# A two-layer decoder trunk: attention steps of a head pair placed inside later projections, and an MLP product with a 512-column operand

## The chip, the cores and the metric

The kernel runs on one core of a Trainium2 chip. The metric is the device time of one execution in microseconds (us); shorter is better. The core's engines work in parallel: TensorE (PE, with its weight loads counted apart as PEld), VectorE (DVE), ScalarE (ACT), GpSimd (POOL) and SyncE (SP), which starts most of the transfers from memory (DMA). Each engine takes its instructions in a fixed order and waits on semaphores for the others.

## The reference

256 tokens (SEQ) of width 1024 (D) pass through two layers. Everything is float32.

```python
def reference(x, ...):
    h = x
    for layer in range(2):
        hn = rms_norm(h, norm_gain[layer, 0])
        if layer == 0:
            h = h + stick_breaking_attention(hn, sb_w_qkv[0], sb_w_o[0])     # 16 heads of 64
        else:
            h = h + nsa_attention(hn, nsa_w_q[0], nsa_gate_b[0], nsa_w_o[0], shared)
        h = h + sqrelu_mlp(rms_norm(h, norm_gain[layer, 1]), mlp_w1[layer], mlp_w2[layer])
        if layer == 0:
            shared = nsa_shared_kv(h, kv_norm, nsa_w_kv, cmp_pos, cmp_w1, cmp_w2)
    return rms_norm(h, final_norm)

def sqrelu_mlp(x, w1, w2):              # w1: 1024 x 4096, w2: 4096 x 1024
    h = relu(x @ w1)
    return (h * h) @ w2

# stick-breaking attention, per head and block of 128 queries
z = q @ k.T * scale
log_1m = where(causal, log_sigmoid(-z), 0)
excl = cumsum(log_1m, reverse=True) - log_1m
a = where(causal, exp(log_sigmoid(z) + excl), 0)
o = a @ v
```

The attention of layer 1 (`nsa_attention`) is a sparse one with three branches: compressed blocks, selected blocks and a window. The change touches it only in how its tiles are allotted.

## The kernel before

**Exact products.** A float32 number is written as a high part, rounded to the type that PE multiplies in one pass, and a low part, the rest. A product of two such numbers is three matmuls, `mm3` (lines 127 to 130): high by high, high by low, low by high. Lines 128, 129 and 130 of the profile are these three. The first operand is the one loaded into PE (a block of 128 x 128), the second streams through it by columns. For projections and the MLP's first product the loaded operand is a weight block and the columns are the 256 tokens, kept transposed in tiles `xh` and `xl` (`xt_tiles` line 196, written by `xt_evac` lines 186 to 194: ACT writes the high part, DVE the low part, for each of eight blocks `k` of 128 rows of D).

**Weights.** All weights are read once, in order, as blocks of up to 1 MB. `fetch` (72) starts a transfer from SP into one of three `raw` buffers. `split` (82) makes half a block ready: an ACT cast (line 92) writes `wh`, a DVE subtraction (line 93) writes `wl`; there are three buffers of each, and after the second half the next block is fetched. `W(i)` waits until block i is split, and calls of `step()` scattered through the code place the splitting of later blocks, up to two blocks ahead. Where a `step()` stands sets where these two instructions (about 1 us each) stand in the order of ACT and DVE.

**Layer 0's attention** (`layer0`, 291 to 427). After the projection of all values `v`, a loop runs over eight head pairs. `proj` (350) makes queries and keys of a pair: 8 blocks k x 2 x `mm3` of 256 columns into one PSUM bank, and a DVE pass that writes `qkT` (line 359). `scores` (362) makes the scores `z` on PE, and then a long chain: two DVE passes clip and mask them into `e` (378, shown as sbe), ACT takes exp (382) and log (383) into `s` (sbs), DVE does a running sum (`tensor_tensor_scan`, 384) and a subtraction (385), and ACT takes the last exp. `turn` (389) transposes the result on PE by 128 x 128 blocks, and ACT (400) and DVE (398) copy one head each into `at` (sbt). `values` (403) multiplies with `v` into `po`, and `o_evac` (199 to 201) writes the high and low part of the output `oT`. The loop's order is written out by hand:

```python
proj(0); scores(0); proj(1); scores(1)
for p in range(NP - 2):
    proj(p + 2); turn(p); scores(p + 2); values(p)
```

`out_proj` (210) follows, the output projection with four weight blocks; its `hooks`, called at a step (i, n, kk), place the last two pairs' turn and values and the first half of the next transposed activations (`xt_tr` 176, `xt_evac`) between its products.

**The MLP** (`mlp`, 229 to 289; used in both layers) goes through 16 chunks of 256 hidden columns. `first(c)` (252) multiplies: 8 blocks k x 2 halves f x `mm3`, 48 matmuls of 256 columns, into one PSUM bank `pu` with the two halves side by side. Then ACT writes relu of it (`mr`, 264), DVE the product of `pu` and `mr` (`ms`, 266), ACT and DVE the high and low part `hh`, `hl` (270, 271). `second` (236) multiplies a chunk by w2: 24 matmuls of 512 columns, into four banks `acc` that stay for the whole MLP. The second product of a chunk follows the first product of the next chunk, so a chunk's result is needed one first product later; the last two chunks' second products come together at the end. In chunk 0 the second half of the transposed activations (blocks k 4 to 7) is only made inside the loop, at k = 2.

**Memory.** Large tiles share six equal buffers of 8 KB per partition (`big`, line 53); PSUM has eight banks in two groups of four (`bank` and `bank2`, lines 56 to 60). The order on each engine is fixed when the program is built: the framework takes the instructions in program order, by dependencies and buffers, and may pull some of them ahead.

Of the kernel before, what the change touches and what calls it, by code (L numbers as in the profile page):

```python
# [7 lines left out]
F32 = mybir.dt.float32  # L8
# [6 lines left out]
P = 128  # L15
# [24 lines left out]
def hybrid_kernel(ctx, tc, x, eye, gcols, gfin, wqk, wv, wo0, wkv, wqa, wqb, wqc, wo1, w1, w2, cw1, cw2, cpos, gate_b, consts, out):  # L40
# [10 lines left out]
        return a.bitcast(F32)  # L51

    def big(shape, dt, name):
        return cp.tile(shape, dt, tag="e", name=name, bufs=6)

    def bank(name, dt=F32):
        return ps.tile([P, 512], dt, tag="a", name=name, bufs=4)
# [1 line left out]
    def bank2(name):  # L59
        return ps.tile([P, 512], F32, tag="z", name=name, bufs=4)  # L60
# [66 lines left out]
    def mm3(o, a, b, first, last):  # L127
        nc.tensor.matmul(o, a[0], b[0], start=first, stop=False, skip_group_check=True)  # L128
        nc.tensor.matmul(o, a[0], b[1], start=False, stop=False, skip_group_check=True)  # L129
        nc.tensor.matmul(o, a[1], b[0], start=False, stop=last, skip_group_check=True)  # L130

    def mm(o, a, b, first, last):
        nc.tensor.matmul(o, a, b, start=first, stop=last, skip_group_check=True)  # L133

    def tok(xt, k, t):
        return xt[0][:, k, t * P:(t + 1) * P], xt[1][:, k, t * P:(t + 1) * P]

    def both(xt, k):
        return xt[0][:, k, :], xt[1][:, k, :]

    def cut(hl, a, b):
        return hl[0][:, a:b], hl[1][:, a:b]
# [51 lines left out]
                                               op0=OP.mult, op1=OP.subtract)  # L194

    def xt_tiles(tag):
        return big([P, NK, T * P], F32R, f"xh{tag}"), big([P, NK, T * P], F32R, f"xl{tag}")

    def o_evac(oT, po, p):
        nc.scalar.copy(oT[0][:, p, :], po[:, 0:T * P])  # L200
# [28 lines left out]
    def mlp(layer, gi, xt, mid, ap):  # L229
# [21 lines left out]

        def first(c):
            w = W(wa[c])
            pu = bank2("pu")
            for k in range(NK):
                if c == 0 and k == 2:
                    xt_evac(xt_tr(1), 1, gi, xt)
                if k % 4 == 0 and (c or k):
                    step()
                for f in range(2):  # L260
                    mm3(pu[:, f * 256:(f + 1) * 256], cut(w, k * 256 + f * P, k * 256 + (f + 1) * P),
                        both(xt, k), f == 0 and k == 0, k == NK - 1)
            r = ap.tile([P, 512], F32, name="mr")
            nc.scalar.activation(r, pu, AF.Relu)
            s = ap.tile([P, 512], F32, name="ms")
            nc.vector.tensor_mul(s, pu, r)  # L266
# [24 lines left out]
    def layer0(ap):  # L291
# [54 lines left out]
        oT = big([P, NP, T * P], F32R, "oT_h"), big([P, NP, T * P], F32R, "oT_l")  # L346

        live = {}

        def proj(p):  # L350
            qk = bank("qk")
            w = W(i_qk[p])
            for k in range(NK):
                if k % 4 == 0:
                    step()
                mm3(qk[:, 0:256], cut(w, k * 256, k * 256 + P), both(xt, k), k == 0, k == NK - 1)
                mm3(qk[:, 256:512], cut(w, k * 256 + P, k * 256 + 2 * P), both(xt, k), False, k == NK - 1)
            qkT = ap.tile([P, 2, T * P], F32, name="qkT", bufs=3)
            nc.vector.tensor_mul(qkT, qk.rearrange("p (a q) -> p a q", a=2), rbq)
            live[p] = qkT  # L360
# [41 lines left out]

        def values(p):
            a = live.pop(p)
            po = bank2("po") if p >= NP - 2 else bank("po")
            for b in range(2):
                for hd in range(2):
                    r = slice(hd * DH, (hd + 1) * DH)
                    cs = slice(p * P + hd * DH, p * P + (hd + 1) * DH)
                    q = (slice(0, 256), slice(256, 384))[b]  # L410
                    mm(po[r, b * P:2 * P], v[:, b, cs], a[:, hd, q], b == 0, b == 1)
            o_evac(oT, po, p)

        proj(0)
        scores(0)
        proj(1)
        scores(1)
        for p in range(NP - 2):
            proj(p + 2)
            turn(p)  # L420
            scores(p + 2)
            values(p)
        xn = xt_tiles("n")
        out_proj(oT, i_o0, {(0, 0, 1): [lambda: turn(NP - 2)], (0, 0, 2): [lambda: values(NP - 2)],
                            (0, 1, 2): [lambda: turn(NP - 1)], (0, 1, 3): [lambda: values(NP - 1)],
                            (1, 1, 2): [lambda: xt_evac(xt_tr(0), 0, 1, xn)]})
        return xn

    def nsa(xk, pt0, ap):
# [14 lines left out]
        kd = [[ap.tile([P, NG, 2, DH], F32, name=f"kd{br}{t}") for t in range(T)] for br in range(2)]  # L444
        vs = [ap.tile([P, 2, 256], F32, name=f"vs{t}") for t in range(T)]
        pts = [pt0]
        rstd = []
# [110 lines left out]
        keys_rope(1)  # L558


        kT = [big([P, NG, 2, T * P], F32R, f"kT{i}") for i in range(2)]
        ph = bank("ph")
        cw_proj(0, 0)
        keys_tr(0)
# [243 lines left out]
        turn(0)  # L808
        cmp_tr(0)
        q_rot(r[2], 10, 6)  # L810
        oT = big([P, NP, T * P], F32R, "oT_h"), big([P, NP, T * P], F32R, "oT_l")
        scores(3)
        scale(2)
        turn(1)
# [141 lines left out]
```

## Time and profile before

| | |
|---|---|
| time, median of 3 runs | 651.77 us (651.48 to 653.22) |
| the profiled execution's own time | 651.07 us |
| span of its instructions | 649.3 us |
| granted TensorE clock, mean | 0.998 |

By stretch of the span, from the busy time of each engine in it (us):

| stretch | length | PE | DVE | ACT |
|---|---|---|---|---|
| start and value projection, to 28.00 | 28.00 | 25.24 | 17.07 | 18.52 |
| layer 0's head pairs, to 99.20 | 71.20 | 67.22 | 57.20 | 41.70 |
| its output projection, to 125.40 | 26.20 | 26.20 | 17.52 | 12.46 |
| first MLP, to 299.00 | 173.60 | 173.60 | 94.68 | 83.29 |
| shared keys and values, layer 1's queries, to 385.00 | 86.00 | 84.71 | 73.44 | 56.36 |
| sparse attention, to 442.00 | 57.00 | 54.00 | 41.60 | 37.09 |
| its output projection, to 462.00 | 20.00 | 20.00 | 11.09 | 8.00 |
| second MLP, to 642.00 | 180.00 | 180.00 | 98.55 | 84.11 |
| last norm and output, to 649.30 | 7.30 | 0.34 | 2.09 | 1.45 |

The profile records one execution, instruction by instruction. An entry such as `L129 PE MATMUL pu<-xln,wh 128*128 128x256` is the matmul of line 129 into tile `pu` from `xl` (of the tile tagged n) and `wh`, with a loaded block of 128 x 128 and 256 columns; `PEld LDWEIGHTS` is the loading of that block. A matmul's recorded duration includes its way through the array and overlaps that of the next one; what a matmul costs is the distance of its start to the next one's start. Rows of the view in order of time give start (us from the span's start), duration, engine, line, operation, tiles and, with `x2` and the like, how many were put together. Windows give start and end, length, then the busy time of PE, PEld, DVE, ACT and POOL with the number of their instructions, the granted clock, the share of DMA and GB/s. A group's line gives, behind its name and count, busy time and mean ns, and then idle time ahead of it.

### The profile page before, as it was taken

The page shows a single profiled execution, that of the slowest core. Times are in us where ns is not written, and L with a number is a line of the kernel's source. Part 1 is how long each engine was busy: PE and PEld are TensorE (multiplying, and loading weights), DVE is VectorE, ACT ScalarE, POOL GpSimd, SP SyncE. Part 2 cuts the span into 40 slices and gives each one's busy share as a digit, 9 for nine tenths or more (in the row PEclk, how much of TensorE's full clock was granted, in tenths as well). Part 3 has the DMA queues.
Part 4 walks back from the last instruction along what each step waited for, and adds up shares of the span by engine and source line. Part 5 has one row for each costly group of instructions (what it writes and reads, how often), then busy time and mean ns, then how long its engine had stood idle before and what let it go on. Part 6 is the DMA issues. An engine that isn't in the chain of part 4 may idle for free.

```text
span 649.3 us, 9971 instructions
## 1 busy us (share of the span) xinstructions
PE 631.3 (97%) x4064; PEld 557.1 (86%) x4064; DVE 413.2 (64%) x574; ACT 343.0 (53%) x564; POOL 57.5 (9%) x100
## 2 busy tenths in 40 slices
PE   8998999999999999999999999999999999999995
PEld 5887887899998989998889986777999989899994
DVE  5678886764555555456899879763765555554544
ACT  5746555564434454444857776752564344544432
POOL 1000000000000000000133354550000000000000
PEclk9999999999999999999999999999999999999999
DMA  8843333355455554553555740101654545555501
GB/s 334 299 174 131 130 130 113 146 189 194 169 189 175 196 187 195 195 193 131 205 194 182 267 149 2 66 1 65 219 197 163 194 174 194 191 195 195 190 6 66
DMA packets 16894, 106.87 MB, mean 165 GB/s; under 512 B 2256, under 2 KB 2512, under 8 KB 4944
## 3 DMA queue, kind: packets, MB, share of 16 engines
q1 hardware_dynamic: 15696, 104.92, 44.1%
q10 hardware_dynamic: 1152, 1.31, 0.7%
q8 instruction: 32, 0.52, 0.3%
q14 instruction: 14, 0.11, 0.0%
HBM read 105.17 MB, written 1.05 MB: 164 GB/s over the span
## 4 chain that ended last, share of the span: by engine, by line
PE 84%; DVE 7%; ACT 3%; issue 2%; POOL 2%; DMA 1%; POOLq 0%; SPq 0%; DVEq 0%; ACTq 0%
PE acc L128 11%; PE acc L129 11%; PE acc L130 11%; PE pu L129 10%; PE pu L130 9%; PE pu L128 9%; PE po L133 3%; PE pk L130 2%; PE pk L129 2%; PE pk L128 2%; DVE wl L93 2%; DVE sbs L384 1%; PE pv L128 1%; PE pv L129 1%; PE pv L130 1%
## 5 line engine op out<-in xcount | busy, mean ns | idle before, releaser
L93 DVE TENSOR_TENSOR wl<-raw,wh 128x1024 fp32r<-128x1024 f32 (+3 forms) x202 | 237.7, 1197 | 178.7 <-ACT wh L92 178.4
L92 ACT CAST wh<-raw 128x1024 fp32r<-128x1024 f32 (+3 forms) x202 | 200.8, 1022 | 199.5 <-issue 103.8
L129 PE MATMUL pu<-xln,wh 128*128 128x256 f32 x512 | 145.0, 283 | 0.0
L130 PE MATMUL pu<-xhn,wl 128*128 128x256 f32 x512 | 144.9, 283 | 0.0
L128 PE MATMUL pu<-xhn,wh 128*128 128x256 f32 x512 | 144.6, 283 | 0.0
L128 PE MATMUL acc<-wh,hh 128*128 128x512 f32 x256 | 100.0, 392 | 0.0
L129 PE MATMUL acc<-wl,hh 128*128 128x512 f32 x256 | 99.7, 391 | 0.0
L129 PEld LDWEIGHTS pu<-xln,wh 128*128 128x128 f32 x512 | 98.1, 192 | 1.4 <-DVE xln L193 0.2
L130 PE MATMUL acc<-wh,hl 128*128 128x512 f32 x256 | 99.2, 389 | 0.0
L128 PEld LDWEIGHTS pu<-xhn,wh 128*128 128x128 f32 x512 | 98.0, 192 | 1.2
L130 PEld LDWEIGHTS pu<-xhn,wl 128*128 128x128 f32 x512 | 98.1, 192 | 0.0
L130 PEld LDWEIGHTS acc<-wh,hl 128*128 128x128 f32 x256 | 48.1, 188 | 10.5 <-DVE hl L271 0.2
L128 PEld LDWEIGHTS acc<-wh,hh 128*128 128x128 f32 x256 | 48.2, 188 | 9.5 <-ACT hh L270 0.5
L129 PEld LDWEIGHTS acc<-wl,hh 128*128 128x128 f32 x256 | 48.2, 188 | 8.8
L128 PE MATMUL qk<-xha,wh 128*128 128x256 f32 x128 | 36.7, 287 | 0.0
L130 PE MATMUL qk<-xha,wl 128*128 128x256 f32 x128 | 36.4, 285 | 0.0
L129 PE MATMUL qk<-xla,wh 128*128 128x256 f32 x128 | 36.2, 283 | 0.0
L747 POOL TENSOR_TENSOR pe<-pe,rs 128x256 f32<-128x256 f32 (+1 forms) x32 | 26.3, 841 | 25.5 <-DVE rs L743 19.8
L270 ACT CAST hh<-ms 128x512 fp32r<-128x512 f32 x32 | 19.9, 622 | 14.5 <-DVE ms L266 14.5
L128 PE MATMUL acc<-wh,oT_h 128*128 128x512 f32 x64 | 25.9, 404 | 0.0
L128 PEld LDWEIGHTS qk<-xha,wh 128*128 128x128 f32 x128 | 24.5, 191 | 0.9 <-issue 0.9
L130 PE MATMUL acc<-wh,oT_l 128*128 128x512 f32 x64 | 25.0, 391 | 0.0
(189 smaller groups left out, 938.2 us busy)
## 6 DMA issues: line engine op xcount, KB each, us to landing
raw<-in_w SPq DMA_DIRECT2D x64, 1024.0 KB, 4.8
raw<-in_wqk SPq DMA_DIRECT2D x8, 1024.0 KB, 5.1
raw<-in_wo SPq DMA_DIRECT2D x8, 1024.0 KB, 4.8
raw<-in_wkv SPq DMA_DIRECT2D x6, 1024.0 KB, 4.7
raw<-in_cw SPq DMA_DIRECT2D x4, 1024.0 KB, 4.8
raw<-in_wv SPq DMA_DIRECT2D x3, 1024.0 KB, 6.4
raw<-in_wqb SPq DMA_DIRECT2D x2, 768.0 KB, 4.1
raw<-in_wqc SPq DMA_DIRECT2D x2, 768.0 KB, 5.6
```

What stands on the lines that cost most here:

```text
L92: nc.scalar.copy(h[:, r], raws[j][:, r])
L93: nc.vector.tensor_sub(lo[:, r], raws[j][:, r], f32(h[:, r]))
L128: nc.tensor.matmul(o, a[0], b[0], start=first, stop=False, skip_group_check=True)
L129: nc.tensor.matmul(o, a[0], b[1], start=False, stop=False, skip_group_check=True)
L130: nc.tensor.matmul(o, a[1], b[0], start=False, stop=last, skip_group_check=True)
L133: nc.tensor.matmul(o, a, b, start=first, stop=last, skip_group_check=True)
L270: nc.scalar.copy(hh, sv)
L384: nc.vector.tensor_tensor_scan(s[:, ::-1], s[:, ::-1], go_on[:, ::-1], 0.0, OP.add, OP.mult)
L747: nc.gpsimd.tensor_tensor(s, s, rs[:, t, :][:, :, None].to_broadcast([P, 2, n]), op=OP.mult)
```

## The change

1. **MLP, first product.** The high and low parts of the transposed activations lie side by side in one tile, [k][high 256, low 256]. `wide` multiplies the high part of a weight block by both in one 512-column matmul and adds the low part of the weight block times the high part in a 256-column matmul: two matmuls in place of three. Each half f has a bank of its own, whose first 256 columns hold high·high + low·high and whose last 256 hold the product with the activations' low part. ACT copies the last 256 columns out, DVE adds them to the first; a DVE pass over both halves then takes max(u, 0)·u. The loop now runs through half 0 and then half 1 (in chunk 0: k 0 to 3 for both halves alternately, then k 4 to 7 for half 0, then for half 1).
2. **Layer 0's head pairs.** Scores, turn and values no longer stand between the projections but inside them: at k = 2 of projection n the scores of pair n − 1 and the values of pair n − 3, at k = 5 the turn of pair n − 2. The hooks of the output projection hold what is left, in the same spirit.
3. **Buffers.** `big` has three buffers in place of six; the paired tiles (transposed activations, `oT`, `kT`) have two of twice the size; the tiles `kd` are one large tile. `values` always uses a bank of the second PSUM group.

```diff
     def big(shape, dt, name):
-        return cp.tile(shape, dt, tag="e", name=name, bufs=6)
+        return cp.tile(shape, dt, tag="e", name=name, bufs=3)
+
+    def pair(shape, name):
+        return cp.tile([P, 2, *shape], F32R, tag="x", name=name, bufs=2)
...
+    def wide(o, a, xt, k, first, last):
+        mm(o, a[0], xt[2][:, k, :, :], first, False)
+        mm(o[:, 0:T * P], a[1], xt[0][:, k, :], False, last)
...
     def xt_tiles(tag):
-        return big([P, NK, T * P], F32R, f"xh{tag}"), big([P, NK, T * P], F32R, f"xl{tag}")
+        xp = cp.tile([P, NK, 2, T * P], F32R, tag="x", name=f"x{tag}", bufs=2)
+        return xp[:, :, 0, :], xp[:, :, 1, :], xp
...
         def first(c):
             w = W(wa[c])
-            pu = bank2("pu")
-            for k in range(NK):
-                if c == 0 and k == 2:
+            pu = [bank2(f"pu{f}") for f in range(2)]
+            r = ap.tile([P, 512], F32, name="mr")
+            u = ap.tile([P, 512], F32, name="mu")
+            s = ap.tile([P, 512], F32, name="ms")
+            ks = [(f, k) for k in range(NK // 2) for f in range(2)] + [(f, k) for f in range(2) for k in range(NK // 2, NK)]
+            for i, (f, k) in enumerate(ks if c == 0 else [(f, k) for f in range(2) for k in range(NK)]):
+                if c == 0 and i == 4:
                     xt_evac(xt_tr(1), 1, gi, xt)
-                if k % 4 == 0 and (c or k):
+                if i % 8 == 0 and (c or i):
                     step()
-                for f in range(2):
-                    mm3(pu[:, f * 256:(f + 1) * 256], cut(w, k * 256 + f * P, k * 256 + (f + 1) * P),
-                        both(xt, k), f == 0 and k == 0, k == NK - 1)
-            r = ap.tile([P, 512], F32, name="mr")
-            nc.scalar.activation(r, pu, AF.Relu)
-            s = ap.tile([P, 512], F32, name="ms")
-            nc.vector.tensor_mul(s, pu, r)
+                wide(pu[f], cut(w, k * 256 + f * P, k * 256 + (f + 1) * P), xt, k, k == 0, k == NK - 1)
+                if k == NK - 1:
+                    q = slice(f * 256, (f + 1) * 256)
+                    nc.scalar.copy(r[:, q], pu[f][:, 256:512])
+                    nc.vector.tensor_add(u[:, q], pu[f][:, 0:256], r[:, q])
+            nc.vector.scalar_tensor_tensor(s, u, 0.0, u, op0=OP.max, op1=OP.mult)
...
-        def proj(p):
+        def proj(p, hooks={}):
...
+                for f in hooks.get(k, ()):
+                    f()
...
-            po = bank2("po") if p >= NP - 2 else bank("po")
+            po = bank2("po")
...
-        proj(0)
-        scores(0)
-        proj(1)
-        scores(1)
-        for p in range(NP - 2):
-            proj(p + 2)
-            turn(p)
-            scores(p + 2)
-            values(p)
+        def inside(n):
+            h = {}
+            if n >= 1:
+                h.setdefault(2, []).append(lambda: scores(n - 1))
+            if n >= 3:
+                h.setdefault(2, []).append(lambda: values(n - 3))
+            if n >= 2:
+                h.setdefault(5, []).append(lambda: turn(n - 2))
+            return h
+
+        for n in range(NP):
+            proj(n, inside(n))
         xn = xt_tiles("n")
-        out_proj(oT, i_o0, {(0, 0, 1): [lambda: turn(NP - 2)], (0, 0, 2): [lambda: values(NP - 2)],
-                            (0, 1, 2): [lambda: turn(NP - 1)], (0, 1, 3): [lambda: values(NP - 1)],
+        out_proj(oT, i_o0, {(0, 0, 1): [lambda: scores(NP - 1), lambda: values(NP - 3)], (0, 0, 3): [lambda: turn(NP - 2)],
+                            (0, 1, 1): [lambda: values(NP - 2)],
+                            (1, 0, 0): [lambda: turn(NP - 1)], (1, 0, 1): [lambda: values(NP - 1)],
                             (1, 1, 2): [lambda: xt_evac(xt_tr(0), 0, 1, xn)]})
```

The rest of the diff gives `oT`, `kT` and `kd` their new tiles (`pair`, and one `big` tile for the four `kd`).

More of the change, by code (lines that the diff above doesn't have):

```diff
@@ L344, in layer0 @@
                 nc.scalar.activation(v[:, t, n * 512:(n + 1) * 512], pv[t][n], AF.Copy, scale=rstd[t])
-        oT = big([P, NP, T * P], F32R, "oT_h"), big([P, NP, T * P], F32R, "oT_l")
+        oT = pair([NP, T * P], "oT")
+        oT = oT[:, 0], oT[:, 1]
         live = {}
-        def proj(p):
+        def proj(p, hooks={}):
             qk = bank("qk")
@@ L443, in nsa @@
         kd0 = big([P, T, 2 * NG, 2, DH], F32, "kd0")
-        kd = [[ap.tile([P, NG, 2, DH], F32, name=f"kd{br}{t}") for t in range(T)] for br in range(2)]
+        kdt = big([P, 2, T, NG * 2 * DH], F32, "kd")
+        kd = [[kdt[:, br, t, :].rearrange("p (g a d) -> p g a d", g=NG, a=2) for t in range(T)] for br in range(2)]
         vs = [ap.tile([P, 2, 256], F32, name=f"vs{t}") for t in range(T)]
@@ L558, in nsa @@
         keys_rope(1)
-        kT = [big([P, NG, 2, T * P], F32R, f"kT{i}") for i in range(2)]
+        kT = pair([NG, 2, T * P], "kT")
+        kT = kT[:, 0], kT[:, 1]
         ph = bank("ph")
@@ L810, in nsa @@
         q_rot(r[2], 10, 6)
-        oT = big([P, NP, T * P], F32R, "oT_h"), big([P, NP, T * P], F32R, "oT_l")
+        oT = pair([NP, T * P], "oT")
+        oT = oT[:, 0], oT[:, 1]
         scores(3)
```

## The prediction, made before the changed kernel was run

> **What bounds the kernel now.** I read the page first, then busy time by stretch of the span, then the order in time of single instructions in the MLP and in layer 0, and last the chain of waits in layer 0. The page says that TensorE (PE) is busy nearly all the time and that the chain that ended last runs mostly through it:
>
> ```profile
> PE 631.3 (97%) x4064; PEld 557.1 (86%) x4064; DVE 413.2 (64%) x574; ACT 343.0 (53%) x564; POOL 57.5 (9%) x100
> PE 84%; DVE 7%; ACT 3%; issue 2%; POOL 2%; DMA 1%; POOLq 0%; SPq 0%; DVEq 0%; ACTq 0%
> ```
>
> That is an average. By stretches (length, then busy time of each engine; first layer 0's attention up to its output projection, then the first MLP, the sparse attention of layer 1, and one MLP chunk):
>
> ```profile
> 28.00:99.20 71.20, 67.22 (x546) 61.17 (x544) 57.20 (x67) 41.70 (x54) 0.54 (x5) 1.00 0.39 148
> 125.40:299.00 173.60, 173.60 (x1131) 159.03 (x1129) 94.68 (x103) 83.29 (x102) 0.00 (x0) 1.00 0.51 185
> 385.00:442.00 57.00, 54.00 (x395) 40.07 (x394) 41.60 (x119) 37.09 (x151) 28.20 (x39) 1.00 0.09 32
> 243.70:254.90 11.20, 11.20 (x74) 10.24 (x73) 5.90 (x7) 5.10 (x6) 0.00 (x0) 1.00 0.48 189
> ```
>
> In the MLP PE never idles, at clock 1.00, and VectorE (DVE) and ScalarE (ACT) are half idle: there the number and the spacing of the products are the time. In layer 0 PE idles 4.0 of 71.2 us, so whatever the change does to waits there can bring at most about 4.0 us.
>
> **MLP first product.** The spacing of the products is read from their starts (start, duration, instruction), across the border from 512-column to 256-column products:
>
> ```profile
> 232.89 0.39 PE L129 MATMUL acc<-wl,hh 128*128 128x512 f32 x1
> 233.11 0.39 PE L130 MATMUL acc<-wh,hl 128*128 128x512 f32 x1
> 233.34 0.28 PE L128 MATMUL pu<-xhn,wh 128*128 128x256 f32 x1
> 233.34 0.19 PEld L129 LDWEIGHTS pu<-xln,wh 128*128 128x128 f32 x1
> 233.45 0.28 PE L129 MATMUL pu<-xln,wh 128*128 128x256 f32 x1
> 233.57 0.28 PE L130 MATMUL pu<-xhn,wl 128*128 128x256 f32 x1
> 233.69 0.28 PE L128 MATMUL pu<-xhn,wh 128*128 128x256 f32 x1
> ```
>
> A 512-column product holds PE 0.227 us (233.34 less 232.89, halved), a 256-column one 0.120 (0.35/3, and 0.120 over the long runs, as the chunk confirms: 48 x 0.120 + 24 x 0.227 = 11.2, the stretch above). So twice the columns cost 0.107 more, and 0.013 is a cost of each product whatever its width. The change computes the same 768 columns for each weight tile with two products in place of three: 0.227 + 0.120 = 0.347 in place of 0.360. There are 512 such groups (32 chunks x 8 k x 2 halves), so PE is relieved of 512 x 0.0133 = 6.8 us; I take 6.9 with the loads' small jitter. Since PE never waits in this stretch, all of it is time.
>
> The Trainium skill (TensorE: Matmul & The Clock Gate, section Back-to-back issue gap) gives the gap of an isolated warm product as columns / 2.4 + 2.5 ns; by it a removed product would save 2.5 ns, an estimate of 512 x 2.5 = 1.3 us in all. The rows above disagree, with 13 ns, and they decide; what would follow if they didn't hold here is a rival below.
>
> What the change adds is the joining of the two halves. Per chunk it takes off one ACT and one DVE pass over the bank and adds two ACT copies, two DVE additions of 256 columns and one DVE pass of 512 from SBUF. Groups (behind the first bar: busy us, mean ns of one):
>
> ```profile
> L266 DVE TENSOR_TENSOR ms<-pu,mr 128x512 f32<-128x512 f32 x32 | 21.9, 683 | 3.0 <-ACT mr L264 2.9
> L264 ACT ACTIVATE mr<-pu 128x512 f32<-128x512 f32 x32 | 19.0, 592 | 3.7 <-PE pu L130 3.7
> L201 DVE TENSOR_TENSOR oT_l<-po,oT_h 128x256 fp32r<-128x256 f32 x16 | 6.7, 417 | 9.3 <-ACT oT_h L200 9.3
> L200 ACT CAST oT_h<-po 128x256 fp32r<-128x256 f32 x16 | 6.0, 375 | 12.7 <-PE po L133 12.6
> ```
>
> DVE: 2 x 0.417 + 0.68 - 0.683 = 0.83 more, so 6.7 of 11.0 us. ACT: 2 x 0.375 - 0.592 = 0.16 more, so 5.3 of 11.0. Both lie under PE, and a chunk's result is used only one first product later (5.5 us). If that cover were gone, 32 x 0.83 = 27 us would show. The final 512-column pass (a maximum and a multiply from SBUF) has no row; between 0.4 and 0.75 it changes nothing. A chunk now takes two PSUM banks of four in place of one: two chunks still fit. At the very end the last chunk's chain is some 0.2 us longer, but the built order keeps 11 or 23 products (2.5 or 5.2 us) of the chunk before it in front: zero, at most 0.3.
>
> In the first chunk there is a cost. Its later four k tiles are being written while PE already multiplies; PE waited 0.16 there before (129.22 plus 0.12, then 129.62):
>
> ```profile
> 129.22 0.40 PE L128 MATMUL pu<-xhn,wh 128*128 128x256 f32 x2
> 129.62 0.38 PE L129 MATMUL pu<-xln,wh 128*128 128x256 f32 x1
> 129.09 0.87 DVE L193 SCALAR_TENSOR_TENSOR xln<-pt,gc,xhn 128x256 fp32r<-128x256 f32 x2
> 130.10 0.88 DVE L193 SCALAR_TENSOR_TENSOR xln<-pt,gc,xhn 128x256 fp32r<-128x256 f32 x2
> ```
>
> The wide product needs both parts at once, and the new loop runs through k = 4 to 7 for one half in 4 x 0.347 = 1.4 us, where it took 2.9 for both halves. The four low parts come at about 129.6, 130.0, 130.6 and 131.0, PE reaches them at 129.1 and then every 0.35: it waits about 0.85 us, 0.6 more than now. In layer 1 the same order meets earlier tiles; I take 0.3. Together 0.9.
>
> **Layer 0.** The rows of the chain of waits (start, length, piece) show that PE is not what paces a head pair:
>
> ```profile
> 77.77 0.98 DVE sbe L385
> ...
> 79.52 1.04 ACT wh L92
> ...
> 80.58 1.23 DVE wl L93
> 81.81 0.94 DVE sbe L378 x2
> ...
> 82.84 0.86 ACT sbs L382
> ...
> 83.72 0.86 ACT sbs L383
> ...
> 84.61 1.78 DVE sbs L384
> ...
> 86.48 0.98 DVE sbe L385
> ```
>
> It is a loop of 8.71 us from subtraction to subtraction: subtraction to the last exponential and on to the weight cast 1.75, cast to the weight's low part (wl) 1.06, wl to the clipping of the scores 1.23, then 1.03, 0.88, 0.89, and scan to subtraction 1.87. PE's own work in a pair is less:
>
> ```profile
> 78.92 0.82 PE L396 MATMUL pa<-ident,sbe 128*128 128x128 f32 x6
> 79.87 0.92 PE L133 MATMUL z<-qkT 64*128 64x256 f32 x8
> 80.98 0.87 PE L133 MATMUL po<-sbt,v 128*64 128x256 f32 x8 [0.19 <-ACT sbt L400]
> 81.78 0.39 PE L128 MATMUL qk<-xha,wh 128*128 128x256 f32 x1
> ```
>
> Transposes 6 x 0.109 = 0.65, scores 0.92, values 0.80, and 48 x 0.120 = 5.76: 8.1 us. Putting scores, turn and values inside the projections hides PE's waits behind projection work, but it moves no work off the ACT and DVE loop, and those engines take their instructions in a fixed order. So what counts is the new order on them. As built, it alternates. In one pair both halves of the next weight are split after the last exponential and ahead of the clipping; in the next, only one half is, and its cast comes before that exponential. In both, the copy of the turned head (sbt) now stands between scan and subtraction, where it was outside the loop:
>
> ```profile
> 71.86 1.23 DVE L93 TENSOR_TENSOR wl<-raw,wh 128x1024 fp32r<-128x1024 f32 x1 [0.21 <-ACT wh L92]
> 73.01 1.02 DVE L378 TENSOR_TENSOR sbe<-z,cst 128x384 f32<-128x384 f32 x2
> 79.12 0.69 DVE L359 TENSOR_TENSOR qkT<-qk,rbq 128x512 f32<-128x512 f32 x1 [0.39 <-PE qk L130]
> 79.78 0.56 DVE L398 COPY sbt<-pa 128x384 f32<-128x384 f32 x1
> ```
>
> Long pair: 8.71 + 1.15 (a second wl, 73.01 less 71.86) + 0.47 (1.78 + 0.56 in place of 1.87) = 10.3. Short pair: subtraction 0.98, qkT 0.66, wl 1.23, 1.03, 0.88, 0.89, scan and copy 2.34 = 8.0, about PE's 8.1. From pair 2's subtraction to pair 5's they come long, short, long: 28.6 against 3 x 8.71 = 26.1, 2.5 later. Behind it PE has less left. Before, from pair 5's subtraction (86.48) to the last scores is 10.8 us:
>
> ```profile
> 97.30 0.92 PE L133 MATMUL z<-qkT 64*128 64x256 f32 x8
> ```
>
> After, the same point (only the last scores, the last values and the output projection left) is reached 0.98 + 0.75 (qkT to scores, 79.87 less 79.12) + 0.92 + 0.80 + 36 x 0.120 + 0.65 = 8.4 later, for the following pair is a short one: 2.4 back. The second pair's scores wait for the same qkT behind the first subtraction on DVE as now, so nothing is gained at the front, and the copy ahead of the second scan costs 0.47. In the output projection the last turns and values need copies that stand behind the last scan; I allow 0.3. Sum for layer 0: 2.5 - 2.4 + 0.5 + 0.3 = 0.9 slower. Bounds: 4.0 gained (all PE idling gone), 3 lost (a long pair in place of each short one, 2.3 each, once more).
>
> **The rest.** The buffers are regrouped (pairs of tiles with two buffers, the large ones with three). Each new owner of a buffer comes after the last reader of the old one in PE's order, so I cost this at zero; a late last reader would show as a wait ahead of the first write. The sparse attention keeps its code, but its built order differs in places. Its stretch above has 3.0 us of PE idling: I take zero, with bounds of 3.0 either way.
>
> **Sum.** The profiled run took 651.07 us (span 649.3 and 1.8 around it), 0.7 under the median 651.77 of the three. 651.07 - 6.9 + 0.9 + 0.9 = 646.0.
>
> **Rivals.** (1) Layer 0 goes at PE's pace after all, because casts come early enough that the loop is 8.0 in each pair: the 4.0 us of idling goes and the 0.9 doesn't come, 651.07 - 6.9 + 0.9 - 4.0 = 641.1. For it speaks PE's 8.1 against 8.7; against it the built order with its long pairs. 0.14. (2) Layer 0 gets worse: one more long pair and the sparse attention's order loses as well, 646.0 + 2.3 + 1.2 = 649.5. 0.14. (3) The 512-column product with two operand parts takes as long as two narrow ones, 0.240, so that a product costs by its columns alone: no gain, 652.9. Against it stands 0.227 for 512 columns in the same stretch. 0.06. (4) Slower: the weight load behind the narrow product. A load is recorded with 0.19 us, and it starts with the product before it. Now every wide product's load has only a 0.120 product to hide behind. If a load couldn't overlap its predecessor, a pair would take 0.227 + 0.19 = 0.417, 0.057 over 0.360: 512 x 0.057 = 29 us, 682. It decides as soon as the narrow product takes over 0.133. Against it: the rows at 233.34 to 233.69, where loads of 0.19 follow each other every 0.12 without a gap. 0.04.
>
> **How the numbers follow.** The forecast has 0.62, with 643 to 649 as its own range. A measurement of this kernel can tell about 0.3% (2 us, so 649.8 and 653.7) from no change. Faster: 0.62, 0.14 and most of rival 2, in all 0.86; same: the rest of rival 2 and rival 3, 0.09; slower: rival 4 and a little beyond, 0.05. The range takes in rivals 1 and 2: 641 to 649.7.
>
> **What would show it.** Right: pairs of starts 0.227 and 0.120 apart in the first products, a chunk of 11.0 us, DVE some 6.7 busy in it; in layer 0 subtractions alternately about 10.3 and 8.0 apart, and the output projection ending within 2 us of now. Wrong: other spacings, gaps on PE within MLP chunks, subtractions evenly 8 us apart, or a sparse attention that is longer or shorter by over 2 us.

## The result, and the profile after

The changed kernel takes 647.28 us (median of 5 runs, 646.07 to 648.71); the kernel before takes 651.77 (5 runs). The ratio is 0.9926, with a 95% interval of 0.9904 to 0.9947: 4.5 us faster. The profiled execution took 646.85 us with a span of 645.0, against 651.07 and 649.3.

The page of the changed kernel, busy times and the chain that ended last:

```profile
PE 626.2 (97%) x3552; PEld 528.3 (82%) x3552; DVE 436.2 (68%) x638; ACT 347.7 (54%) x596; POOL 58.4 (9%) x100
PE 80%; DVE 9%; ACT 3%; issue 2%; POOL 2%; DMA 2%; POOLq 0%; SPq 0%; ACTq 0%; DVEq 0%
```

PE has exactly 512 matmuls fewer (4064 less 3552), but only 5.1 us less busy time. The busy time by stretch, one MLP chunk from its first matmul to that of the next, and layer 0's head pairs:

```profile
243.60:254.70 11.10, 11.10 (x57) 9.41 (x56) 6.67 (x9) 5.26 (x7) 0.00 (x0) 1.00 0.51 185
28.00:99.20 71.20, 66.69 (x542) 61.54 (x542) 55.43 (x65) 42.09 (x55) 0.54 (x5) 1.00 0.42 149
```

The chunk takes 11.11 us, forecast 11.0, before 11.22; PE is busy all through it, and DVE's 6.67 and ACT's 5.26 are the forecast 6.7 and 5.3. Layer 0 still leaves PE idle for 4.5 us. Inside the chunk, matmuls in order of time (start, duration, instruction):

```profile
243.62 0.39 PE L137 MATMUL pu<-xn,wh 128*128 128x512 f32 x1
243.84 0.28 PE L137 MATMUL pu<-xn,wl 128*128 128x256 f32 x1
243.96 0.40 PE L137 MATMUL pu<-xn,wh 128*128 128x512 f32 x1
244.19 0.28 PE L137 MATMUL pu<-xn,wl 128*128 128x256 f32 x1
244.31 0.40 PE L137 MATMUL pu<-xn,wh 128*128 128x512 f32 x1
```

The first wide one takes 0.227 to the next start; from then on a pair takes 0.35. From the second pair of a chunk on the mean is 0.3533 us (0.236 from wide to narrow, 0.117 from narrow to wide), where 0.347 was forecast and three narrow ones took 0.360: half of the gain is there.

Layer 0, the chain of waits over a short and a long pair (start, length, piece):

```profile
71.30 0.95 DVE sbe L404
72.26 0.61 DVE qkT L378
...
72.91 0.92 PE z L137 x8
73.84 0.82 PE po L137 x8
...
74.68 0.29 ACT oT L211
...
75.02 0.87 ACT sbs L401
...
75.91 0.86 ACT sbs L402
...
76.79 1.77 DVE sbs L403
...
78.93 0.97 DVE sbe L404
...
80.68 1.04 ACT wh L96
...
81.74 2.36 DVE wl L97 x2
84.10 0.94 DVE sbe L397 x2
...
89.03 0.96 DVE sbe L404
```

Subtractions (L404) lie 7.6 and 10.1 us apart in turn. In the long pair both wl stand between the cast and the clipping; in the short one the chain goes from the subtraction straight to queries and keys and on through PE's scores and values and ACT's copy of the output (`oT`, done at 74.97). DVE's clippings, which the prediction counted there, are done at 74.92 and so end level with it.

Stages, worked out from the starts of the matmuls in the two profiles (us):

| stage | before | after | difference |
|---|---|---|---|
| start to the first queries and keys | 30.94 | 31.28 | +0.34 |
| to the end of layer 0's output projection | 90.92 | 90.58 | -0.34 |
| first products of the first MLP's first two chunks | 12.64 | 12.71 | +0.07 |
| rest of that MLP, to the shared keys and values | 169.15 | 167.45 | -1.70 |
| sparse attention, from the queries to its output projection | 88.65 | 87.53 | -1.12 |
| first products of the second MLP's first two chunks | 12.44 | 12.71 | +0.27 |
| to its last 48 matmuls | 157.08 | 155.50 | -1.58 |
| from there to the end | 18.11 | 17.85 | -0.26 |

The other stages agree within 0.02, and the sum is the difference of the spans, 4.3.

### The profile page after: what moved, and what is told of

Its sections match the earlier page's. It is cut to its first block, busy times and chain, and to the rows that moved or that the text cites. A ratio compares the mean times of both kernels' runs of the same rounds, so it can differ in the third digit from the quotient of the medians.

```text
span 645.0 us, 9058 instructions
## 1 busy us (share of the span) xinstructions
PE 626.2 (97%) x3552; PEld 528.3 (82%) x3552; DVE 436.2 (68%) x638; ACT 347.7 (54%) x596; POOL 58.4 (9%) x100
## 4 chain that ended last, share of the span: by engine, by line
PE 80%; DVE 9%; ACT 3%; issue 2%; POOL 2%; DMA 2%; POOLq 0%; SPq 0%; ACTq 0%; DVEq 0%
PE pu L137 27%; PE acc L132 11%; PE acc L133 11%; PE acc L134 11%; DVE wl L97 3%; PE po L137 2%; PE pk L134 2%; PE pk L132 2%; PE pk L133 2%; DVE sbs L403 2%; ACT wh L96 1%; DMA raw<-in_wv 1%; PE z L137 1%; PE pq L132 1%; PE pq L133 1%
## 5 line engine op out<-in xcount | busy, mean ns | idle before, releaser
L137 PE MATMUL pu<-xn,wh 128*128 128x512 f32 x512 | 182.2, 399 | 0.6 <-DVE xn L203 0.6
L137 PE MATMUL pu<-xn,wl 128*128 128x256 f32 x512 | 143.0, 281 | 0.0
L137 PEld LDWEIGHTS pu<-xn,wh 128*128 128x128 f32 x512 | 95.9, 188 | 24.2 <-DVE xn L203 1.2
L137 PEld LDWEIGHTS pu<-xn,wl 128*128 128x128 f32 x512 | 96.7, 189 | 1.5
L280 ACT COPY mr<-pu 128x256 f32<-128x256 f32 x64 | 23.6, 369 | 28.4 <-PE pu L137 28.4
L132 PE MATMUL qk<-xa,wh 128*128 128x256 f32 x128 | 37.3, 291 | 0.0
L134 PE MATMUL qk<-xa,wl 128*128 128x256 f32 x128 | 36.3, 284 | 0.0
L133 PE MATMUL qk<-xa,wh 128*128 128x256 f32 x128 | 36.2, 283 | 0.0
L281 DVE TENSOR_TENSOR mu<-pu,mr 128x256 f32<-128x256 f32 x64 | 26.7, 418 | 5.0 <-ACT mr L280 5.0
L132 PE MATMUL acc<-wh,oT 128*128 128x512 f32 x64 | 25.9, 405 | 0.0
L132 PEld LDWEIGHTS qk<-xa,wh 128*128 128x128 f32 x128 | 24.5, 191 | 1.0 <-issue 0.9
```

Source lines behind the costliest of these rows:

```text
L280: nc.scalar.copy(r[:, q], pu[f][:, 256:512])
L281: nc.vector.tensor_add(u[:, q], pu[f][:, 0:256], r[:, q])
```

## The experiments

All times are medians, beside runs of the kernel before on the same chip; the last column is the ratio to it.

| kernel | us | ratio (95%) |
|---|---|---|
| changed kernel | 647.28 | 0.9926 (0.9904 to 0.9947) |
| e1, only layer 0 and the buffers | 650.36 | 0.9978 (0.9968 to 0.9987) |
| e2, only the MLP and the buffers | 647.66 | 0.9939 (0.9926 to 0.9953) |
| e3, matmuls grouped by width | 645.63 | 0.9905 (0.9894 to 0.9917) |
| e4, even head pairs | 642.02 | 0.9855 (0.9840 to 0.9869) |
| e5, only the buffers | 650.23 | 0.9988 (0.9978 to 0.9998) |
| e6, half the weight load | 644.87 | 0.9896 (0.9880 to 0.9911) |
| e7, long pairs throughout | 648.38 | 0.9945 (0.9932 to 0.9958) |
| e8, even pairs and grouped matmuls | 639.86 | 0.9819 (0.9806 to 0.9832) |

### The two halves of the change apart: e1 and e2

e1 puts the MLP's `first` back as it was before (three matmuls, one bank):

```diff
-                wide(pu[f], cut(w, ...), xt, k, k == 0, k == NK - 1)
+                mm3(pu[:, f * 256:(f + 1) * 256], cut(w, ...), both(xt, k), f == 0 and k == 0, k == NK - 1)
```

> The changed kernel with the MLP's first product put back to three 256-column matmuls and one bank; layer 0's order and the buffers stay as changed. Theory A (the gain is the MLP's matmuls; layer 0's new order is worth nothing): chunks 11.21 us apart as in the kernel before, the output projection of layer 0 ends at 121.9 us as in both kernels, and the sparse attention keeps its 1.1 us gain because that comes with the tiles and the order built around them: 651.8 - 1.1 = 650.7 us. Rival B (the new order of layer 0 carries part of the gain, hidden in the comparison by something that the wide product costs there): about 649 us, layer 0 ending before 121 us. Rival C (the 1.1 us of the sparse attention belong to the MLP): 651.8 us.

e2 puts layer 0's loop and the hooks behind it back (and the bank that `values` writes):

```diff
-        for n in range(NP):
-            proj(n, inside(n))
+        proj(0); scores(0); proj(1); scores(1)
+        for p in range(NP - 2):
+            proj(p + 2); turn(p); scores(p + 2); values(p)
```

> The changed kernel with layer 0's loop and the hooks of its output projection put back; wide product and buffers stay as changed. Theory A: subtractions 8.7 us apart again in place of 10.1 and 7.6 in turn, layer 0's output projection ends at 121.9 us all the same, and the whole takes 647.3 us as the changed kernel does, within 0.5. Rival B (long pairs cost what they seem to, 1.4 us each over 8.7, and the short ones don't pay it back): 645 us or less.

e1 took 650.36, e2 647.66 us. In e1 the chunks are 11.22 apart again, and from the first queries and keys to the end of layer 0's output projection it is 90.59, as in the changed kernel; in e2 that stage takes 90.90, as before. So layer 0's new order is worth 0.3 us, although its pairs take 7.6 and 10.1 us in place of 8.7. The wide product is worth 3.1 (e1's 650.36 less 647.28); what is left comes with the buffers, as e5 below shows. Theory A holds in both.

### What the new pairs cost: e4 and e7

e4 forces the order of DVE and ACT; `issue_after` puts what its block holds behind an instruction on the same engine. The last exponential goes behind the cast of the next half, one wl behind queries and keys, the other behind the clippings:

```diff
             # scores(p), after the two clippings (the last of them is sb)
+            with tc.issue_after(sb.ins):
+                step()
             nc.scalar.activation(s, e, AF.Exp)
...
-            nc.scalar.activation(e, e, AF.Exp)
+            cast.append(split_h())                       # only the cast of a half
+            with tc.issue_after(cast[0][0].ins):
+                nc.scalar.activation(e, e, AF.Exp)
...
             # proj(p), after queries and keys (mq); its own step() only for p == 0
+            with tc.issue_after(mq.ins):
+                split_l(*cast.pop())                     # its low part
```

> The changed kernel with the order of DVE and ACT in layer 0 forced: in each pair queries and keys, one half's low part (wl), the two clippings, the other half's low part, scan, copy and subtraction; the cast for the first half is put ahead of the last exponential. No work is added or left out. Theory A (layer 0 is paced by the order on DVE and ACT, long pairs are those that do both wl ahead of the clippings): subtractions evenly about 8.1 us apart, PE's own pace in place of 10.1 and 7.6 in turn, layer 0's output projection ends 3 to 4 us earlier (118 to 119 us), 643.5 to 644.5 us. Rival B (a wait for PE's scores or for the casts takes its place): pairs 8.7 us or more apart, the output projection ends at 121 to 122 us, 647 us.

642.02 us, 5.3 less than the changed kernel. DVE of e4 in order of time, a pair from subtraction to subtraction, and then the window of 25 us (60 to 85) in e4, in the changed kernel and in the kernel before:

```profile
67.01 0.96 DVE L419 TENSOR_TENSOR sbe<-sbe,sbs 128x774 f32<-128x774 f32 x1
67.95 0.69 DVE L388 TENSOR_TENSOR qkT<-qk,rbq 128x512 f32<-128x512 f32 x1
68.56 1.22 DVE L100 TENSOR_TENSOR wl<-raw,wh 128x1024 fp32r<-128x1024 f32 x1
70.23 1.03 DVE L410 TENSOR_TENSOR sbe<-z,cst 128x384 f32<-128x384 f32 x2 [0.46 <-PE z L146]
71.17 1.22 DVE L100 TENSOR_TENSOR wl<-raw,wh 128x1024 fp32r<-128x1024 f32 x1
72.30 0.42 DVE L221 TENSOR_TENSOR oT<-po,oT 128x256 fp32r<-128x256 f32 x1
73.13 1.77 DVE L418 TENSOR_TENSOR_SCAN sbs<-sbs,go_on 128x774 f32<-128x774 f32 x1 [0.40 <-ACT sbs L417]
74.81 0.53 DVE L437 COPY sbt<-pa 128x384 f32<-128x384 f32 x1
75.26 0.96 DVE L419 TENSOR_TENSOR sbe<-sbe,sbs 128x774 f32<-128x774 f32 x1
```

```profile
60.00:85.00 25.00, 25.00 (x215) 23.16 (x214) 22.43 (x28) 15.89 (x22) 0.32 (x3) 1.00 0.35 126
```

```profile
60.00:85.00 25.00, 23.10 (x197) 21.11 (x196) 20.60 (x27) 13.53 (x18) 0.22 (x2) 1.00 0.33 124
```

```profile
60.00:85.00 25.00, 24.28 (x206) 21.99 (x205) 21.57 (x28) 15.56 (x21) 0.33 (x3) 1.00 0.32 124
```

The pairs in the middle take 8.24 to 8.28 (the first two 7.6, the last two 8.9 and 9.4, with more splitting of weights in them). PE never idles in this window, and now DVE waits for PE's scores (0.46) where PE waited for DVE. The stage to the end of layer 0's output projection takes 86.32 in place of 90.58, and PE idles for 0.45 us in all of it, where it idled for 4.5. So with this order the new placement runs at PE's pace; what held it up was the built order of DVE and ACT, alternating between two patterns.

e7 makes nearly each pair long by placing scores and values at k = 3 and turn at k = 6:

```diff
-                h.setdefault(2, []).append(lambda: scores(n - 1))
+                h.setdefault(3, []).append(lambda: scores(n - 1))
```

> The changed kernel with scores and values at k = 3 and turn at k = 6 of a projection, by which the built order does both halves' wl ahead of the clippings in nearly each pair, with one cast ahead of the last exponential and one behind it. Theory A (a pair is paced by the chain subtraction, last exponential, casts behind it, wl, clipping, exponential, logarithm, scan, copy, subtraction): one cast less in it than in the long pairs of the changed kernel, 10.1 - 0.93 = 9.2 us for each pair; over five pairs 46 in place of 44 to 45, so layer 0's output projection ends about 1 to 1.5 us later than 121.9, 648.5 us. Rival B (PE's position of the scores decides, one block later than now): pairs alternate as before or go at 8.7, 647.3 us.

648.38 us; from the third pair on the subtractions lie 8.97 apart (9.2 expected; only the last spacing is 7.4), and the stage takes 91.26, 0.7 longer than in the changed kernel (1 to 1.5 expected). The chain goes as theory A says, through one cast and one wl more than in a short pair, 0.2 us a pair shorter than worked out:

```profile
70.79 0.97 DVE sbe L404
...
71.78 0.85 ACT sbe L405
72.63 0.94 ACT wh L96
...
73.60 1.23 DVE wl L97
74.82 0.94 DVE sbe L397 x2
...
79.76 0.97 DVE sbe L404
```

### Where half of the MLP's gain went: e3 and e6

e3 issues, for each half of a chunk except the first chunk, its eight wide matmuls and then its eight narrow ones:

```diff
-                wide(pu[f], cut(w, ...), xt, k, k == 0, k == NK - 1)
+                mm(pu[f], cut(w, ...)[0], xt[2][:, k, :, :], k == 0, False)
+                if k == NK - 1:
+                    for j in range(NK):
+                        mm(pu[f][:, 0:T * P], cut(w, ... j ...)[1], xt[0][:, j, :], False, j == NK - 1)
```

> The changed kernel, but in every chunk except the first the eight 512-column matmuls of a half come first and then its eight 256-column ones. In the changed kernel the two alternate and a pair takes 0.353 us where 0.227 + 0.120 = 0.347 was forecast. Theory A (the missing 6 to 7 ns belong to the change from narrow to wide, a weight load that has only a narrow matmul to hide behind): the wide ones go at 0.227 and the narrow ones at 0.120, except next to a change; 4 changes for 16 pairs of a chunk, a chunk 11.03 to 11.06 us in place of 11.11, so about 1.5 to 2.4 us less: 645.3 us. Rival B (the wide matmul itself takes 0.236, because its columns are two operand parts or because it fills a bank of 512 that the narrow one then adds to): wide ones 0.236 apart, a chunk 11.1 us or more, 647.3 us.

645.63 us. A chunk takes 11.03 us; its first products in order of time:

```profile
231.49 1.98 PE L138 MATMUL pu<-xn,wh 128*128 128x512 f32 x8
233.31 1.12 PE L138 MATMUL pu<-xn,wl 128*128 128x256 f32 x8
234.26 2.00 PE L138 MATMUL pu<-xn,wh 128*128 128x512 f32 x8
236.10 1.12 PE L138 MATMUL pu<-xn,wl 128*128 128x256 f32 x8
237.05 0.40 PE L133 MATMUL acc<-wh,hh 128*128 128x512 f32 x1
```

Eight wide ones behind wide ones take 1.82 (0.227 each), eight behind narrow ones 1.84. Looked at singly over the chunks, the first five wide matmuls behind a run of narrow ones take 0.233, 0.236, 0.229, 0.232 and 0.231, together some 0.027 more than five of 0.2267 each, then 0.227; the first narrow one behind a wide one takes 0.113 in place of 0.120. So the wide matmul with two operand parts is as quick as any other (rival B falls), and each change to narrow matmuls and back costs some 20 ns in all (the expectation for e8 below counts 23). The changed kernel pays 6.7 ns (0.3533 less 0.3467) at each step from one pair to the next, and the 20 ns once a chunk, where the second products begin; the kernel before pays those there too.

e6 asks whether it is the weight load. The narrow matmul loads 64 of 128 weight columns; half of the hidden units go without the low weight part:

```diff
-        mm(o[:, 0:T * P], a[1], xt[0][:, k, :], False, last)
+        mm(o[0:64, 0:T * P], a[1][:, 0:64], xt[0][:, k, :], False, last)
```

> The changed kernel, but the 256-column matmul of the low weight part loads only 64 of its 128 weight columns, so that half of the hidden units go without that term (left out). Number and width of the streamed columns stay. Theory A (what a pair takes beyond 0.347 us is the weight load, which takes about as long as a narrow matmul and so puts the next wide one late): with half the load a pair takes 0.347 or less, down to 0.340 if the narrow one follows a wide one after 0.113 each time; chunk 10.9 to 11.0 us, 643.5 to 645.5 us. Rival B (the change between widths costs it, or adding into half of a bank that was just filled): pairs stay at 0.353, 647.3 us.

644.87 us, a chunk of 11.01:

```profile
231.20:242.21 11.01, 11.01 (x57) 8.57 (x56) 6.68 (x9) 5.26 (x7) 0.00 (x0) 1.00 0.57 194
```

A pair takes 0.3467 us (0.2292 + 0.1175), the forecast figure, with the same count and width of streamed columns in the same alternation. So the change between widths doesn't by itself make the pair longer, and that part of rival B falls. What makes it longer goes with the 128 loaded columns of the narrow matmul, or else with its full output, for e6 writes half the partitions too; the two weren't told apart. Nor does e6 show how. Its matmuls and their loads (PEld) in order of time:

```profile
231.42 0.28 PE L137 MATMUL pu<-xn,wl 128*64 128x256 f32 x1
231.43 0.19 PEld L137 LDWEIGHTS pu<-xn,wh 128*128 128x128 f32 x1
231.54 0.40 PE L137 MATMUL pu<-xn,wh 128*128 128x512 f32 x1
231.54 0.14 PEld L137 LDWEIGHTS pu<-xn,wl 128*64 128x64 f32 x1
```

The load that starts behind a narrow matmul is that of the next wide one, and it is still whole (0.19); the halved load starts behind a wide matmul, which covers it either way. So theory A's picture, a load that has only a narrow matmul to hide behind, isn't what e6 changed, and it stays unproven. And where e6's second products begin, the first five wide matmuls are late as in every other run, by some 0.027 together. The Trainium skill (TensorE: Matmul & The Clock Gate, section LDWEIGHTS) gives a load as columns / 1.2 ns, an estimate of 107 ns for 128 columns and 53 for 64. The trace agrees on the difference, 0.188 us recorded for a load of 128 columns and 0.134 to 0.138 for one of 64; that a pair waits for a load of that length no run here shows.

### The buffers, and what is scatter: e5, e9 and e10

e5 is the kernel before with the tiles of the changed one (`pair`, three `big` buffers, one tile for `kd`).

> The kernel before with only the buffers regrouped as in the changed kernel (pairs of tiles, three large buffers, one tile for kd); layer 0's order and the MLP as before. Theory A (the buffers are worth nothing by themselves): 651.8 us within 0.6; from the first queries and keys to the end of layer 0's output projection 90.9 us, chunks 11.21, the stretch of the sparse attention somewhere between 87.5 and 89.3, where the five profiles with the changed tiles lie that have all the same order there. Rival B (the 1.4 us that layer 0's order and the buffers gained together without the MLP come mostly from the buffers, since layer 0 shows only 0.3): 650.8 us, with the last stretch, from the last products' start to the end, at 17.8 in place of 18.1.

650.23 us, ratio 0.9988 (0.9978 to 0.9998): rival B's figure of 650.8 is nearer, at the edge of what can be told. The stage to the end of layer 0's output projection takes 90.90, a chunk 11.22, the stage from the last 48 matmuls to the end 17.84, and the first products of the second MLP's first two chunks take 12.64 with the old product, 0.2 more than in the kernel before. That 0.2, and the shorter end, come with the tiles and the order built around them.

e9 and e10 are the kernel before, unchanged; they took 654.17 and 653.49 us, one run each, beside one more of 653.09.

> The kernel before, unchanged, profiled once more. The comparison of the first two profiles shows the sparse attention (first query products to output projection) 1.1 us shorter after the change, 87.5 in place of 88.65. Theory A (scatter between executions; the nine profiles with the changed tiles, all with one built order there, lie between 87.5 and 89.3 us): another value than 88.65 by 0.3 us or more, within 87.4 to 89.4; the start up to the first queries and keys also differs by some 0.3 from 30.94. Rival B (the order built before the change holds it at 88.65): 88.5 to 88.8 again.

> The same kernel a further time, for the same question: theory A, a third value for the sparse attention, 87.4 to 89.4 us; rival B, 88.5 to 88.8 us. The last stretch, from the start of the last products to the end, is 18.1 us in the first profile and 17.8 to 17.9 in all nine with the changed tiles: 18.1 again if the tiles shorten it, 17.8 if that too was scatter.

The sparse attention, first in the kernel before (first profile, then e10, then e9), then in the changed kernel (window, length, busy times, and the granted clock third from the end):

```profile
352.94:441.59 88.65, 85.23 (x611) 69.71 (x609) 67.90 (x168) 57.76 (x189) 38.18 (x57) 1.00 0.30 104
```

```profile
354.73:444.00 89.27, 85.28 (x611) 69.71 (x609) 67.99 (x168) 57.60 (x189) 38.86 (x57) 1.00 0.30 103
```

```profile
354.57:444.59 90.02, 87.79 (x610) 72.20 (x609) 68.73 (x168) 57.80 (x189) 38.51 (x57) 0.96 0.29 103
```

```profile
351.33:438.86 87.53, 84.11 (x611) 69.13 (x609) 67.69 (x168) 57.91 (x189) 39.07 (x57) 1.00 0.31 111
```

Neither theory was right as put. The stretch does scatter, in good part by the granted clock: in five of the twelve profiles (e1, e2, e3, e8, e9) the clock is halved for 3.4 or 6.8 us of this stretch, and such a profile is 0.1 to 1.8 us longer there than those with the same tiles at full clock. In e9 that is this window:

```profile
390.80:397.60 6.80, 6.80 (x37) 6.01 (x36) 6.09 (x19) 5.20 (x20) 2.31 (x3) 0.50 0.00 1
```

At clock 1.00 the kernel before has 88.65 and 89.27, and the five such profiles with the new tiles have 87.50 to 87.88 (the changed kernel, e4 to e7). So 0.8 to 1.8 us come with the new tiles. With them comes another order of the instructions in this stretch, the same one in all five; that the order makes the difference is likely, but no run has the one without the other. Two profiles on the one side are few, but e5's time says the same: its five executions at a mean granted clock of 0.997 or more took 649.6 to 650.2 us, and the eight of the kernel before beside them 650.7 to 652.0. The last stage is 18.1 in all three profiles of the kernel before and 17.8 to 17.9 in all nine with the new tiles. Taken together, 1.2 us by the tiles (e5's difference of medians; its interval allows 0.1 to 1.4), 0.3 by layer 0's order and about 3.1 by the wide product make 4.6, and the measured difference is 4.5. Of the last stage and of the sparse attention it stays open which instruction makes the difference. The start up to the first queries and keys lies between 30.7 and 32.8 with no pattern by kernel.

### Both improvements together: e8

e8 has e4's order in layer 0 and puts all sixteen wide matmuls of a chunk ahead of its sixteen narrow ones, the joining of the halves behind both:

```diff
-                wide(pu[f], cut(w, ...), xt, k, k == 0, k == NK - 1)
+                mm(pu[f], cut(w, ...)[0], xt[2][:, k, :, :], k == 0, False)       # both f, all k
...
+            for f, k in fk:
+                mm(pu[f][:, 0:T * P], cut(w, ...)[1], xt[0][:, k, :], False, k == NK - 1)
```

> The changed kernel with the forced order in layer 0 and, in every chunk but the first, all sixteen 512-column matmuls ahead of all sixteen 256-column ones, so that only one change from narrow to wide is left in a chunk; nothing is left out. In layer 0 the first half's wl now also comes behind queries and keys. Theory A (the two gains are in different stretches and add up; each change from narrow to wide costs 23 ns): 642.0 - 1.7 - 0.7 = 639.6 us, chunk 11.00 us. Rival B (the joining of the halves now comes at the end for both, so the second products or PSUM banks wait for it): chunk over 11.05 us with PE idle ahead of the second products, 641 us or more.

639.86 us: 1.8% faster than the kernel before, and 7.4 us faster than the changed one. (The order in layer 0 is e4's; there too the first wl came behind queries and keys.) The chunk:

```profile
227.20:238.20 11.00, 11.00 (x57) 9.42 (x56) 6.67 (x8) 5.16 (x7) 0.00 (x0) 1.00 0.54 189
```

One change from narrow to wide is left in it, the one to the second products, where e3 has two. The gains add up as theory A has it (639.6 expected).

## Why the prediction was right, and where its terms were off

The forecast was 646.0 for the profiled kind of execution (own range 643 to 649); it took 646.85, and the median is 647.28. That the total came out this close is luck: the largest term was off by half, and others that went better than forecast, or weren't forecast at all, made up for most of it:

- **MLP products, forecast -6.9.** The mechanism held: the saving is a fixed cost per matmul, and it shows in full in a stretch where PE never waits. The size was off by half. The term took spacings of wide next to wide and of narrow next to narrow, and none of the rows showed a wide one regularly behind a narrow one. Chunks follow each other by 11.107 us in place of 11.220. Sixteen pairs at 13.3 ns would save 0.213; the fifteen steps from one pair to the next cost 0.100 of it, which leaves 7 ns a pair (0.113 / 16): 512 x 7 = 3.6 us. The prediction's weight-load rival looked at the right place, the step from narrow to wide, with a threshold too coarse: narrow matmuls in a row showed no gap, but the first five wide ones behind them come late. Whether the load is the reason stays open (e6). The kernel before had this step too, once a chunk: behind 48 narrow ones it spent 0.233, 0.236, 0.229, 0.232 and 0.231 on the first five second products. The other rule that the prediction quotes, that of the Trainium skill (TensorE: Matmul & The Clock Gate, section Back-to-back issue gap), by which 1.3 us would be saved, is not borne out either: the saving was 3.6, between the two.
- **First chunks, forecast +0.9.** The waits in them grew by 0.73, 0.31 in the first MLP and 0.42 in the second; the table's +0.34 is less because the first products of four chunks save their 0.4 there as well. Of the second MLP's part 0.2 is there with the old product too (e5). The one long wait in the first MLP is 0.47 us (129.04 and 0.12, then 129.63), about 0.3 more than before where 0.6 was forecast; from then on there is hardly any waiting, for the built order doesn't go through the four tiles of one half in a row (later rows have two wide matmuls, then two narrow ones). In the second MLP 0.3 was put in because the tiles came earlier there; in the changed kernel they don't, and the same wait of 0.47 stands there.

```profile
129.04 0.28 PE L137 MATMUL pu<-xn,wl 128*128 128x256 f32 x1
129.63 0.50 PE L137 MATMUL pu<-xn,wh 128*128 128x512 f32 x1 [0.31 <-DVE xn L203]
```

- **Layer 0, forecast +0.9.** Measured -0.34. The alternation was right: 10.1 and 7.6 against 10.3 and 8.0. From pair 2's subtraction to pair 5's it took 27.8 us (28.6 forecast), 1.7 more than before; behind it 2.5 came back (2.4 forecast); at the front 0.5 was lost as forecast; the 0.3 allowed for the output projection didn't come. The error in the pairs, 0.8, is half the short pair (7.62 for 8.0) and half the two long ones (0.2 each). In both, DVE steps were added up at their full durations, and they overlap a little at their ends: scan and copy take 2.14 to the next subtraction where 2.34 was put in, and in the short pair the step behind the subtraction starts after 0.87 of its 0.95. The 0.5 at the front is right in size but not in place: it comes in two parts, 0.23 and 0.31, in the first two pairs, where one copy of 0.47 ahead of the second scan was put in.
- **Sparse attention and buffers, forecast 0, with 3.0 either way.** About -1.1 and, at the very end, -0.3 came with the new tiles. The prediction saw that the order of the sparse attention differed and left it unpriced.

Rival 1 (layer 0 at PE's pace, 4.0 less) didn't come, and for the reason given, the built order; e4 shows that it was one forced order away: 4.3 us less in that stage. (Against the kernel before it is 4.6, a little over the bound of 4.0 that the prediction read from PE's idle time.) Rivals 2, 3 and 4 didn't come; e3 rules 3 out by the wide matmul's 0.227 among its like.

## What to carry to other kernels

Work that is put elsewhere in the program pays only if the other engines' instruction order lets it: read that order pair by pair, and if it alternates between patterns, price each and force the short one. When matmuls of two widths alternate, don't add up their prices from runs of one width; issue them in groups by width, which left nothing out and won back 0.08 to 0.10 of 11.1 us a chunk here. And before a difference of 1 us in one stage is called a gain or a loss, compare the granted clock in that stage and profile the old kernel more than once.

## What the runs showed of the hardware

Behind narrow matmuls (256 columns, 0.120 apart among themselves) the first five of a run of wide ones (512 columns, 0.227) are together some 0.027 us late, even though PE shows no idle time. It is the same behind 48 of them (the kernel before), 16 (e8), 8 (e3) and a single one (the changed kernel), and behind a narrow one with half the weight columns (e6). The matmul behind the first narrow one follows 0.007 early, after 0.113. Halving the loaded weight columns of the narrow one, and with them its output, made a pair of both widths 0.3467 instead of 0.3533. And the granted clock was 0.50 for 6.8 us of the sparse attention in one execution (e9) and 1.00 throughout that stretch in another of the same program on the same chip (e10).
